# Attention scores of a two-layer trunk: from 128-row products of a stacked query to 64-row products on the two row halves of TensorE's array

## The chip, the cores and the metric

The kernel runs on one core of one Trainium2 chip. The metric is the device time of one execution in microseconds; a kernel's time is the median of its runs. The engines are TensorE (PE, with its weight loads listed apart as PEld), VectorE (DVE), ScalarE (ACT), GpSimd (POOL) and SyncE (SP), which issues the DMAs.

## The reference

Two layers on x of 1024 positions by 1024 channels. Each layer computes x + W_out(mixer(RMSNorm(x)) * silu(gate)), and one input projection gives q, k, v and the gate. Layer A is sliding-window attention (16 query heads, 2 key heads, window 128, a sink per head). Layer B runs three dilated sliding windows, (window, dilation) = (128,1), (512,4), (2048,16), each with 16 query heads and 4 key heads of its own, and merges them by their softmax denominators. Heads have 64 dims. The scores are, in blocks of 128 positions, queries of a block against keys of the block and of the one before it:

```python
s = jnp.einsum('nbqgrd,nbkgd->nbgrqk', qb, kk, preferred_element_type=jnp.float32) * SCALE
valid = (dist >= 0) & (dist <= max_dist) & ((blk > 0) | (j >= BLOCK))
p = jnp.exp(s - m[..., None])
```

## The kernel before

All matrix products run in float32r, with every operand split into a high part (rounded to float32r) and a low part (the rest), so that a product of two float32 operands becomes three float32r products (high·high, high·low, low·high): `mm3`, line 434. Transposes run in float32 on TensorE against an identity.

**Units.** The attention is made of 128 units, one for four query heads of one key head and one block of 128 positions: 32 in layer A (four groups of heads `n`, eight blocks) and 96 in layer B (four groups `n`, three dilations `g`, eight blocks). 72 of them see two key blocks (256 keys) and 56 see one (128 keys): the first block of a sequence, and all units of dilation 16, where two sequences of 64 share a block. A unit is `prep` (line 482: norm, rotation on POOL, transposes into `pq`, splitting of query and key) and `attend` (line 528: scores, softmax, transposes of the probabilities into `ptt`, product with v into `po`).

**Scores.** `prep` writes the query into `qs` with the high part of a head in partitions 0 to 63 and its low part in 64 to 127, by two ACT and two DVE instructions on 64 partitions each (even heads, odd heads). The key `kd` (`akr` in layer A, `kring` in layer B) holds the same 64 dims twice, in both partition halves, once as a high and once as a low copy. So a product with 128 rows gives (q_high + q_low)·k, and two of them, with k_high and k_low, give the score. With two key blocks these are two matmuls of 256 columns into one PSUM region. With one key block there is a single matmul of 256 columns, high and low copy side by side, and a DVE addition (`pe<-pss,con`) adds one half to the mask before the reduction reads the other. The tile `pss` is one PSUM bank and holds two heads; each unit takes two of them in turn (`NB["pS"]` is 2). A DVE reduction per head (listed as CUSTOM_DVE) adds the mask, scales and takes the minimum of the negated scores; ACT takes the exponential.

**What sets the order.** `Plan` (line 97) records all instructions in program order with an estimated duration from `_cost` (line 245), and `issue` (line 191) then orders them by a list scheduler: on each engine, of the instructions whose operands are there by its estimate, the one earliest in program order (with biases). The projections (`psz`, `psg` for the gate, `psw` for W_out) thus fill what the attention leaves of TensorE. Every instruction is issued from one recording helper, line 286, so all rows of the profile bear that line, and tiles tell them apart.

Of the kernel before, what the change touches and what calls it, by code (L numbers as in the profile page):

```python
# [12 lines left out]
F32 = mybir.dt.float32  # L13
F32R = mybir.dt.float32r
AF = mybir.ActivationFunctionType
OP = mybir.AluOpType
AX = mybir.AxisListType.X

P = 128
# [4 lines left out]
HD = 64  # L24
# [29 lines left out]
NB = {"pz": 2, "pS": 2, "pT": 2, "pO": 1, "pM": 1}  # L54
# [40 lines left out]


class Plan:
    """Records the instructions in program order, then issues them engine by engine in the order
    that a list scheduler finds: of the instructions whose operands are there, the earliest in
    program order first, so that the projections fill what the attention leaves of TensorE."""  # L100

    ENGINES = ("PE", "ACT", "DVE", "POOL", "SP")
    LAT = {("PE", "PE"): 0, ("PE", "ACT"): 200, ("PE", "DVE"): 200, ("PE", "POOL"): 200, ("PE", "SP"): 200,
# [141 lines left out]
def _cost(eng, name, out, ins):  # L245
    n = out.free_size()
    if eng == "PE":
        if name == "transpose":
            return 109
        return 213 if n < 2 * P else n / 2.4 + 3  # L250
    if eng == "SP":
        return out.size() * 4 / 300.0
    if eng == "DVE":
        if name == "tensor_reduce":
            n = ins[0].free_size()
        if name == "reciprocal":
            return 60 + 6.5 * n
        if name == "tensor_scalar":
            return 130 + 0.53 * n
        return (140 if name in ("tensor_tensor_reduce", "scalar_tensor_tensor") else 70) + 1.04 * n  # L260
    if eng == "ACT":
        return (60 if len(ins) == 1 else 160) + 0.84 * n
    return 150 + 2.1 * n
# [27 lines left out]
def trunk(ctx, tc, x, norm_a, w_in_a, q_gain_a, k_gain_a, sinks_a, w_out_a,  # L291
          norm_b, w_in_b, q_gain_b, k_gain_b, w_out_b, xt, const, out):
    nc = Plan(tc)
    x, out = x[0], out[0]
# [11 lines left out]
    pS = pool("ps", NB["pS"], space=PS)  # L306
# [4 lines left out]
    def f(ap):  # L311
        return ap.bitcast(F32)

# [1 line left out]
    ident = nc.tile(cp, [P, P], F32, name="ident")  # L315
    make_identity(tc.nc, ident)
    con = nc.tile(cp, [P, CS_W + 6 * P], F32, name="con")
# [7 lines left out]
    rows = nc.tile(sp, [16, P], F32, tag="zi", bufs=3, name="rows")  # L325
# [19 lines left out]
    gc = gt[:, 16:24].rearrange("p (a b) -> p a b", a=2)  # L345
# [22 lines left out]
    x1d = tc.dram_tile([T, D], F32, name="x1d")  # L368
    xpd = tc.dram_tile([T, D], F32, name="xpd")

# [1 line left out]
    def split(hi, lo, src, g=None, sub=nc.vector):  # L372
        if g is None:
            nc.scalar.activation(hi, src, AF.Copy)
            sub.tensor_tensor(lo, src, f(hi), op=OP.subtract)
        else:
            nc.scalar.activation(hi, src, AF.Copy, scale=g)
            nc.vector.scalar_tensor_tensor(lo, src, g, f(hi), op0=OP.mult, op1=OP.subtract)
# [103 lines left out]
    def prep(kind, order, tpos, z, nh, kv, slot):  # L482
        w = nh * HD
        sq = nc.tile(sp, [P, 320], F32, tag="sq", bufs=1, name="sq")
        nc.gpsimd.tensor_tensor(sq[:, :w], z[:, :w], z[:, :w], op=OP.mult)
        ss = nc.tile(sp, [P, 5], F32, tag="ss", bufs=2, name="ss")
        nc.vector.tensor_reduce(ss[:, :nh], sq[:, :w].rearrange("p (h d) -> p h d", d=HD), axis=AX, op=OP.add)
        r = nc.tile(sp, [P, 5], F32, tag="r", bufs=3, name="r")
        rstd(r[:, :nh], ss[:, :nh], 1.0, HD * EPS)
        zr = z[:, :w].rearrange("p (h d) -> p h d", d=HD)[:, :, :ROT]  # L490
        t0 = nc.tile(sp, [P, 5, ROT], F32, tag="t0", bufs=1, name="t0")[:, :nh]
        t1 = nc.tile(sp, [P, 5, ROT], F32, tag="t1", bufs=1, name="t1")[:, :nh]
        nc.gpsimd.tensor_tensor(t0, zr, rg[:, kind, :nh], op=OP.mult)
        c_, s_ = cs[:, order, tpos, 0], cs[:, order, tpos, 1]
        nc.gpsimd.tensor_tensor(t1, t0, c_[:, None, :].to_broadcast([P, nh, ROT]), op=OP.mult)
        hf = ROT // 2
        nc.gpsimd.tensor_tensor(zr[:, :, :hf], t0[:, :, hf:],
                                s_[:, None, :hf].to_broadcast([P, nh, hf]), op=OP.mult)
        nc.gpsimd.tensor_tensor(zr[:, :, hf:], t0[:, :, :hf],
                                s_[:, None, hf:].to_broadcast([P, nh, hf]), op=OP.mult)  # L500
        nc.gpsimd.tensor_tensor(zr, zr, t1, op=OP.add)
        pm = nc.tile(pM, [P, 4, P], F32, tag="m", bufs=NB["pM"], name="pq")
        for pr in range(2):
            nc.tensor.transpose(pm[:, pr], z[:, pr * P:(pr + 1) * P], ident)
        qs = nc.tile(sp, [P, 2, 2, P], F32R, tag="qs", bufs=2, name="qs")
        gq = gc[:, 0, kind:kind + 1]
        for two in range(2):
            rows = slice(two * HD, two * HD + HD)
            nc.scalar.activation(qs[:HD, :, two], pm[rows, 0:2], AF.Copy, scale=gq[rows])
            nc.vector.scalar_tensor_tensor(qs[HD:, :, two], pm[rows, 0:2], gq[rows], f(qs[:HD, :, two]),  # L510
                                           op0=OP.mult, op1=OP.subtract)
        if kv is not None:
            kd, vt = kv
            kh, kl = kd[:, 0], kd[:, 1]
            kk = nc.tile(sp, [P, 2, HD], F32, tag="kk", bufs=2, name="kk")
            nc.gpsimd.tensor_scalar(kk, z[:, None, 4 * HD:5 * HD].to_broadcast([P, 2, HD]), r[:, 4:5], -8.0,
                                    op0=OP.mult, op1=OP.mult)
            nc.tensor.transpose(pm[:, 2], kk.rearrange("p a b -> p (a b)"), ident)
            gk = gc[:, 1, kind:kind + 1]
            nc.scalar.activation(kh[:, slot], pm[:, 2], AF.Copy, scale=gk)  # L520
            nc.vector.scalar_tensor_tensor(kl[:, slot], pm[:, 2], gk, f(kh[:, slot]),
                                           op0=OP.mult, op1=OP.subtract)
            zv = z[:, 5 * HD:6 * HD]
            nc.scalar.activation(vt[:, slot, :HD], zv, AF.Copy)
            nc.gpsimd.tensor_tensor(vt[:, slot, HD:], zv, f(vt[:, slot, :HD]), op=OP.subtract)
        return qs, r

    def attend(qs, r, kv, slots, mask, nm, l, sink, o_even, o_odd):
        flush()
        kd, vt = kv  # L530
        nb = len(slots)
        W = nb * P
        if nb == 2:
            st = slots[1] - slots[0]
            ks = [kd[:, s, slots[0]:slots[1] + 1:st] for s in range(2)]
        pe = nc.tile(sp, [P, 4, 2 * P], F32, tag="p", bufs=2, name="pe")
        for pr in range(2):
            ps = nc.tile(pS, [P, 2, 2 * P], F32, tag="s", bufs=NB["pS"], name="pss")
            for two in range(2):
                if nb == 2:  # L540
                    nc.tensor.matmul(ps[:, two], qs[:, pr, two], ks[0], start=True, stop=False)
                    nc.tensor.matmul(ps[:, two], qs[:, pr, two], ks[1], start=False, stop=True)
                else:
                    nc.tensor.matmul(ps[:, two], qs[:, pr, two], kd[:, :, slots[0]], start=True, stop=True)
            if nb == 1:
                nc.vector.tensor_tensor(pe[:, 2 * pr:2 * pr + 2, P:], ps[:, :, P:],
                                        mask[:, None, :].to_broadcast([P, 2, P]), op=OP.add)
            for two in range(2):
                h = 2 * pr + two
                nc.vector.tensor_tensor_reduce(out=pe[:, h, :W], in0=ps[:, two, :W],  # L550
                                               in1=mask if nb == 2 else pe[:, h, P:], op0=OP.add,
                                               op1=OP.min, scale=r[:, h:h + 1], scalar=3e38,
                                               accum_out=nm[:, h:h + 1])
        if sink is not None:
            nc.vector.tensor_tensor(nm, nm, sink, op=OP.min)
        for h in range(4):
            nc.scalar.activation(pe[:, h, :W], pe[:, h, :W], AF.Exp, bias=nm[:, h:h + 1], scale=-1.0,
                                 accum_out=l[:, h:h + 1])
# [11 lines left out]
        for two, dst in ((0, o_even), (1, o_odd)):  # L570
            for d, sl in dst:
                a = po[:HD].rearrange("p (pr two q) -> p pr two q", pr=2, two=2)[:, :, two]
# [80 lines left out]
            nc.sync.dma_start(zi[sl, :width], view(zd))  # L653
        return zi

    # ================= layer A =================
    hT = [alloc_h(j) for j in range(4)]
    hB = {}

# [87 lines left out]
    for n in range(4):  # L747
# [5 lines left out]
        if n == 0:  # L753
            zd = tc.dram_tile([T, width], F32, name="za0")
            for t in range(NT):
# [12 lines left out]
                pr = nc.tile(pM, [P, 4, P], F32, tag="m", bufs=NB["pM"], name="pr")  # L768
# [8 lines left out]
            pr = nc.tile(pM, [P, 4, P], F32, tag="m", bufs=NB["pM"], name="pr")  # L777
# [13 lines left out]
        if n == 3:  # L791
            nc.bias = WOA
            y = load_y(0, 0, range(4), sub=YA)
# [5 lines left out]
        for t in range(NT):  # L799
# [7 lines left out]
            qs, r = prep(0, 0, t, z, 5 if n % 2 == 0 else 4, kv if n % 2 == 0 else None, t)  # L807
            sk = nsink[:, 4 * n:4 * n + 4]
            nm = nc.tile(sp, [P, 4], F32, tag="nm", bufs=2, name="nm")
            l = nc.tile(sp, [P, 4], F32, tag="l", bufs=2, name="l")  # L810
            slots = [t - 1, t] if t else [0]
            mask = mask_a[:, P:3 * P] if t else mask_a[:, :P]
# [15 lines left out]
    w0 = out_a_whole((6, 7))  # L828
    hT = hB

    # ================= layer B =================
    kk = nc.tile(sp, [P, 2, 4, P], F32R, tag="v2", bufs=1, name="kring")
    kring = [kk, nc.tile(sp, [P, 4, P], F32R, name="vring")]
    ucount = [0]
# [86 lines left out]
    for n in range(4):  # L921
        og, stn = {}, {}
        for g in (2, 1, 0):
            w = w0 if n == 0 and g == 2 else w_b(g, n)
            zd = bounce(hT, w, 384, f"zb{g}_{n}")
            if g == 0 and n == 3:
# [6 lines left out]
                y = first_y(0)  # L933
# [63 lines left out]
```

## Time and profile before

| | before |
|---|---|
| median of 3 runs | 1298.51 us (1296.77 to 1298.76) |
| span of the profiled execution | 1295.1 us |
| PE busy | 1257.3 us, 97%, 7851 matmuls |
| PEld busy | 1132.2 us, 87% |
| DVE busy | 1032.6 us, 80% |
| ACT busy | 867.9 us, 67% |
| POOL busy | 703.6 us, 54% |

A matmul's duration in the profile runs from its start to its modelled end, and matmuls overlap, so durations add up to more than the engine's time. What a matmul costs the stream is the distance from its start to the start of the next one. In the timeline view, equal instructions in a row stand as one row with their count.

### The profile page before, as it was taken

What the parts mean: (1) busy time and instruction counts of PE and PEld (TensorE: products, weight loads), DVE (VectorE), ACT (ScalarE), POOL (GpSimd) and SP (SyncE); (2) the same over time, 40 slices, a digit from 0 to 9 for tenths busy, and PEclk for the clock granted to TensorE, in tenths of its full rate; (3) what the DMA queues carried; (4) which work ended last, traced back from release to release, by engine and by line L of the source; (5) the groups of instructions that cost most, each with busy time, mean ns of one, the idle gap of its engine ahead of it and who ended that gap; (6) DMA issues with size and microseconds to landing.
All of it is one profiled execution on the core that took longest, in us unless ns stands there. A gap on an engine that the chain in (4) does not pass through costs nothing. (4 is left out here: it accounts for less than half of the span.)

```text
span 1295.1 us, 25655 instructions
## 1 busy us (share of the span) xinstructions
PE 1257.3 (97%) x7851; PEld 1132.2 (87%) x7851; DVE 1032.6 (80%) x2968; ACT 867.9 (67%) x2365; POOL 703.6 (54%) x1388
## 2 busy tenths in 40 slices
PE   6999999999999999999999999999999999999998
PEld 5999999998778999988889988889988888887777
DVE  8778778777965338778888888988778888779995
ACT  4376766767653347877757877767877767887760
POOL 4764455446410046555577656577556566587621
PEclk9999999999999999999999999999999999999999
DMA  7423223346254133223334323334223344354544
GB/s 242 128 76 110 77 85 102 91 161 185 83 166 142 66 112 100 82 62 105 117 112 128 88 74 94 107 106 137 82 69 106 98 124 133 117 156 135 165 141 157
DMA packets 142666, 149.74 MB, mean 116 GB/s; under 512 B 33576, under 2 KB 129344, under 8 KB 142528
## 3 DMA queue, kind: packets, MB, share of 16 engines
q1 hardware_dynamic: 142528, 148.09, 37.3%
q8 instruction: 63, 1.03, 0.3%
q14 instruction: 75, 0.61, 0.2%
HBM read 105.57 MB, written 42.47 MB: 114 GB/s over the span
## 5 line engine op out<-in xcount | busy, mean ns | idle before, releaser
L286 PE MATMUL psz<-wt,hT 128*128 128x384 f32 (+1 forms) x3072 | 640.9, 344 | 6.1 <-ACT wt L286 3.9
L286 PEld LDWEIGHTS psz<-wt,hT 128*128 128x128 f32 x3072 | 512.9, 191 | 14.8 <-ACT wt L286 4.0
L286 PE MATMUL psg<-hT,wt 128*128 128x256 f32 x1536 | 226.0, 291 | 0.0
L286 ACT ACTIVATE pe<-pe,st 128x128 f32<-128x128 f32 (+1 forms) x384 | 169.5, 443 | 59.8 <-DVE st L286 57.4
L286 PEld LDWEIGHTS psg<-hT,wt 128*128 128x128 f32 x1536 | 203.9, 192 | 2.7
L286 PE MATMUL ptt<-ident,pe 128*128 128x128 f32 x800 | 177.3, 281 | 6.2 <-ACT pe L286 5.4
L286 DVE SCALAR_TENSOR_TENSOR qs<-pq,gt,qs 64x256 fp32r<-64x256 f32 x256 | 123.8, 484 | 42.4 <-ACT qs L286 36.0
L286 POOL TENSOR_TENSOR r<-r,ex 128x5 f32<-128x5 f32 (+1 forms) x128 | 152.8, 1194 | 5.9
L286 ACT ACTIVATE qs<-pq,gt 64x256 fp32r<-64x256 f32 x256 | 120.1, 469 | 46.2 <-PE pq L286 41.0
L286 DVE TENSOR_TENSOR pp<-ptt,pp 128x512 fp32r<-128x512 f32 x200 | 131.7, 685 | 20.9 <-ACT pp L286 18.1
L286 POOL TENSOR_TENSOR sq<-zi 128x320 f32<-128x320 f32 (+1 forms) x128 | 93.4, 730 | 88.0 <-DMA zi<-zb 41.1
L286 PEld LDWEIGHTS ptt<-ident,pe 128*128 128x128 f32 x800 | 104.6, 140 | 39.8 <-ACT pe L286 23.6
L286 DVE CUSTOM_DVE_ANT_0 pe<-pss,con,r 128x256 f32<-128x256 f32 x288 | 127.7, 476 | 10.5 <-PE pss L286 8.7
L286 ACT ACTIVATE oh<-po 64x512 f32<-64x512 f32 x128 | 76.1, 595 | 81.3 <-PE po L286 79.8
L286 DVE SCALAR_TENSOR_TENSOR wt<-raw,gt,wt 128x384 fp32r<-128x384 f32 (+1 forms) x188 | 109.9, 615 | 23.8 <-ACT wt L286 22.6
L286 POOL TENSOR_SCALAR r<-ss 128x5 f32<-128x5 f32 (+1 forms) x128 | 31.1, 243 | 179.3 <-DVE st L286 96.4
L286 ACT ACTIVATE pp<-ptt 128x512 fp32r<-128x512 f32 x200 | 111.5, 594 | 19.2 <-PE ptt L286 18.0
L286 PE MATMUL po<-pp,vring 128*128 128x512 f32 x280 | 107.7, 413 | 2.4 <-DVE pp L286 1.8
L286 PE MATMUL psw<-hT,wy 128*128 128x512 f32 x384 | 105.7, 405 | 0.0
L286 ACT ACTIVATE wt<-raw,gt 128x384 fp32r<-128x384 f32 (+1 forms) x188 | 100.0, 564 | 6.4 <-PE psw L286 2.4
L286 PE MATMUL pss<-kring,qs 128*128 128x256 f32 x560 | 94.3, 285 | 0.8 <-DVE kring L286 0.6
L286 PEld LDWEIGHTS pss<-kring,qs 128*128 128x128 f32 x560 | 84.4, 188 | 9.8 <-DVE kring L286 3.1
(142 smaller groups left out, 2115.6 us busy)
## 6 DMA issues: line engine op xcount, KB each, us to landing
raw<-in_w_in_b_dram SPq DMA_DIRECT2D x96, 192.0 KB
zb<-z SPq DMA_DIRECT2D x96, 192.0 KB
cb<-cd SPq DMA_DIRECT2D x128, 128.0 KB
zi<-zb SPq DMA_DIRECT2D x64, 192.0 KB
raw<-in_w_in_a_dram SPq DMA_DIRECT2D x48, 128.0 KB
yraw<-yd SPq DMA_DIRECT2D x24, 256.0 KB
zi<-zb SPq DMA_DIRECT2D x64, 96.0 KB
xt<-in_xt_dram SPq DMA_DIRECT2D x16, 256.0 KB
```

The lines of the kernel that those rows point to most:

```text
L286: self.plan.add(self.name, method, lambda: fn(*args, **kw), outs, ins, dur, func)
```

## The change

- `prep`: the high parts of all four heads go into `qs[:, 0]` and the low parts into `qs[:, 1]`, by one ACT and one DVE instruction on 128 partitions. An even head lies in partitions 0 to 63, an odd one in 64 to 127.
- `attend`: a head's score is three products with 64 rows: (q_high, k_high), (q_high, k_low), (q_low, k_high). Even and odd head alternate, on rows 0 to 63 and on rows 64 to 127, and write different `pss` tiles (`ps[two]`, which now holds the even or the odd heads of both pairs). With one key block a product has 128 columns, with two 256. The DVE addition of the one-block units is gone. Both `pss` tiles of a unit are taken before its first product.
- `_cost`: a matmul's estimate is max(108, n/2.4 + 13) instead of n/2.4 + 3 (213 under 256 columns). The orders below follow from this too.

Matmuls go from 7851 to 8587: 800 of the scores become 1536, 672 with 128 columns and 864 with 256, half of them with a tile of 64 rows at row 0 and half at row 64.

```diff
@@ _cost
-        return 213 if n < 2 * P else n / 2.4 + 3
+        return max(108, n / 2.4 + 13)
@@ prep
-        gq = gc[:, 0, kind:kind + 1]
-        for two in range(2):
-            rows = slice(two * HD, two * HD + HD)
-            nc.scalar.activation(qs[:HD, :, two], pm[rows, 0:2], AF.Copy, scale=gq[rows])
-            nc.vector.scalar_tensor_tensor(qs[HD:, :, two], pm[rows, 0:2], gq[rows], f(qs[:HD, :, two]),
-                                           op0=OP.mult, op1=OP.subtract)
+        split(qs[:, 0], qs[:, 1], pm[:, 0:2], gc[:, 0, kind:kind + 1])
@@ attend
-        if nb == 2:
-            st = slots[1] - slots[0]
-            ks = [kd[:, s, slots[0]:slots[1] + 1:st] for s in range(2)]
+        st = slots[-1] - slots[0] or 1
+        ks = [kd[:, i, slots[0]:slots[-1] + 1:st] for i in range(2)]
         pe = nc.tile(sp, [P, 4, 2 * P], F32, tag="p", bufs=2, name="pe")
+        ps = [nc.tile(pS, [P, 2, 2 * P], F32, tag="s", bufs=NB["pS"], name="pss") for _ in range(2)]
         for pr in range(2):
-            ps = nc.tile(pS, [P, 2, 2 * P], F32, tag="s", bufs=NB["pS"], name="pss")
-            for two in range(2):
-                if nb == 2:
-                    nc.tensor.matmul(ps[:, two], qs[:, pr, two], ks[0], start=True, stop=False)
-                    nc.tensor.matmul(ps[:, two], qs[:, pr, two], ks[1], start=False, stop=True)
-                else:
-                    nc.tensor.matmul(ps[:, two], qs[:, pr, two], kd[:, :, slots[0]], start=True, stop=True)
-            if nb == 1:
-                nc.vector.tensor_tensor(pe[:, 2 * pr:2 * pr + 2, P:], ps[:, :, P:],
-                                        mask[:, None, :].to_broadcast([P, 2, P]), op=OP.add)
...
+            for i, (x, y) in enumerate(((0, 0), (0, 1), (1, 0))):
+                for two in range(2):
+                    rows = slice(two * HD, two * HD + HD)
+                    nc.tensor.matmul(ps[two][:, pr, :W], qs[rows, x, pr], ks[y][rows], start=i == 0, stop=i == 2)
+        for h in range(4):
+            nc.vector.tensor_tensor_reduce(out=pe[:, h, :W], in0=ps[h % 2][:, h // 2, :W], in1=mask, op0=OP.add,
+                                           op1=OP.min, scale=r[:, h:h + 1], scalar=3e38,
+                                           accum_out=nm[:, h:h + 1])
```

On PE, the scores of the unit of layer A with n = 2 and t = 4 (two key blocks) stand like this before; `psz` is the projection of the next group, `pc` a transpose of 8 columns, `po` the product of the unit ahead with v:

```order
L286 MATMUL pss<-akr,qs 128x256 x2
L286 MATMUL psz<-wt,hT 128x256 x2
L286 MATMUL pc<-ident,rc 8x128
L286 MATMUL pss<-akr,qs 128x256 x2
L286 MATMUL po<-pp,akv 128x512
L286 MATMUL pss<-akr,qs 128x256 x4
```

and like this now (the pattern goes on to the twelfth score product):

```order
L286 MATMUL pss<-akr,qs 128x256
L286 MATMUL psg<-hT,wt 128x256
L286 MATMUL pc<-ident,rc 8x128
L286 MATMUL pss<-akr,qs 128x256
L286 MATMUL psg<-hT,wt 128x256
L286 MATMUL pss<-akr,qs 128x256
L286 MATMUL psg<-hT,wt 128x256
L286 MATMUL pss<-akr,qs 128x256
L286 MATMUL psg<-hT,wt 128x256
```

The eight score products stood in three stretches; the twelve now stand singly, each between two gate products of 128 rows.

On PE, the scores of the unit of layer B with n = 0, g = 1 and u = 4 (one key block) before, and what stands around them:

```order
L286 MATMUL psz<-wt,hT 128x384
L286 MATMUL po<-pp,vring 128x512
L286 MATMUL psz<-wt,hT 128x384
L286 MATMUL pss<-kring,qs 128x256 x4
L286 MATMUL pq<-ident,zi 128x128 x2
L286 MATMUL psz<-wt,hT 128x384 x14
```

and the same unit now:

```order
L286 MATMUL ptt<-ident,pe 128x128 x2
L286 MATMUL pss<-kring,qs 128x128 x2
L286 MATMUL psg<-hT,wt 128x256 x2
L286 MATMUL pss<-kring,qs 128x128 x4
L286 MATMUL po<-pp,vring 128x512
L286 MATMUL pss<-kring,qs 128x128 x5
L286 MATMUL po<-pp,vring 128x512 x2
L286 MATMUL pss<-kring,qs 128x128
L286 MATMUL po<-pp,vring 128x512
```

Four products in one stretch have become twelve of 128 columns in four stretches, with `psg` and `po` of 128 rows between them. Over the whole program PE's order has 232 stretches of score products before and 405 now, of which 93 are a single product, 117 have two, 64 four and 53 five.

## Rows read from the trace of the kernel before

**Rows 1.** The page, part 1 (busy, share, instructions) and part 2 (granted clock).
```profile
PE 1257.3 (97%) x7851; PEld 1132.2 (87%) x7851; DVE 1032.6 (80%) x2968; ACT 867.9 (67%) x2365; POOL 703.6 (54%) x1388
PEclk9999999999999999999999999999999999999999
```

**Rows 2.** Groups by shape, PE: tiles, shapes, count, busy us, mean ns, idle before.
```profile
L286 PE MATMUL psz<-wt,hT 128*128 128x384 f32 x2688 | 584.7, 351 | 6.1 <-ACT wt L286 3.9 <-DVE wt L286 1.9 <-ACT z L286 0.2
L286 PE MATMUL psg<-hT,wt 128*128 128x256 f32 x1536 | 226.0, 291 | 0.0
L286 PE MATMUL ptt<-ident,pe 128*128 128x128 f32 x800 | 177.3, 281 | 6.2 <-ACT pe L286 5.4
L286 PE MATMUL po<-pp,vring 128*128 128x512 f32 x280 | 107.7, 413 | 2.4 <-DVE pp L286 1.8 <-DVE og L286 0.4
L286 PE MATMUL psw<-hT,wy 128*128 128x512 f32 x384 | 105.7, 405 | 0.0
L286 PE MATMUL pss<-kring,qs 128*128 128x256 f32 x560 | 94.3, 285 | 0.8 <-DVE kring L286 0.6
...
L286 PE MATMUL psz<-wt,hT 128*128 128x256 f32 x384 | 56.2, 289 | 0.0
...
L286 PE MATMUL pss<-akr,qs 128*128 128x256 f32 x240 | 43.9, 295 | 2.1 <-DVE akr L286 0.6 <-DVE qs L286 0.6 <-ACT pe L286 0.6
```

**Rows 3.** Timeline, PE, layer A: start us, length, tiles, count; projections up to a transpose.
```profile
34.17 1.73 PE L286 MATMUL psz<-wt,hT 128*128 128x384 f32 x9
35.73 0.27 PE L286 MATMUL pr<-ident,sr 128*128 128x128 f32 x1
```

**Rows 4.** Timeline, PE, layer A: gate products, with an 8-column transpose (pc) among them.
```profile
206.42 0.27 PE L286 MATMUL pc<-ident,rc 128*8 128x128 f32 x1
206.45 0.96 PE L286 MATMUL psg<-hT,wt 128*128 128x256 f32 x6
207.24 0.39 PE L286 MATMUL po<-pp,akv 128*128 128x512 f32 x1
207.47 0.28 PE L286 MATMUL psg<-hT,wt 128*128 128x256 f32 x1
207.59 0.38 PE L286 MATMUL pq<-ident,zi 128*128 128x128 f32 x2
207.73 0.60 PE L286 MATMUL psg<-hT,wt 128*128 128x256 f32 x3
208.16 0.63 PE L286 MATMUL po<-pp,akv 128*128 128x512 f32 x2
```

**Rows 5.** Timeline, PE, layer B: the four score products of a one-block unit.
```profile
711.48 0.64 PE L286 MATMUL pss<-kring,qs 128*128 128x256 f32 x4
711.95 0.38 PE L286 MATMUL pq<-ident,zi 128*128 128x128 f32 x2
```

**Rows 6.** Timeline, PE then PEld: the transpose with 16 rows (pg) among projections.
```profile
48.44 1.03 PE L286 MATMUL psz<-wt,hT 128*128 128x384 f32 x5
49.40 0.23 PE L286 MATMUL pg<-ident,rows 16*128 16x16 f32 x1
49.56 0.96 PE L286 MATMUL psz<-wt,hT 128*128 128x384 f32 x4
50.36 0.27 PE L286 MATMUL pr<-ident,ra 128*8 128x128 f32 x1
...
49.40 0.13 PEld L286 LDWEIGHTS pg<-ident,rows 16*128 16x128 f32 x1 [0.25 <-issue]
49.56 0.64 PEld L286 LDWEIGHTS psz<-wt,hT 128*128 128x128 f32 x4
```

**Rows 7.** Groups by shape, ACT and DVE: what the change removes or halves.
```profile
L286 ACT ACTIVATE qs<-pq,gt 64x256 fp32r<-64x256 f32 x256 | 120.1, 469 | 46.2 <-PE pq L286 41.0 <-DVE qs L286 1.5
...
L286 DVE SCALAR_TENSOR_TENSOR qs<-pq,gt,qs 64x256 fp32r<-64x256 f32 x256 | 123.8, 484 | 42.4 <-ACT qs L286 36.0
...
L286 DVE TENSOR_TENSOR pe<-pss,con 128x256 f32<-128x256 f32 x112 | 43.8, 417 | 15.9 <-PE pss L286 15.8
```

More of the change, by code (lines that the diff above doesn't have):

```diff
@@ L532, in attend @@
         W = nb * P
-        if nb == 2:
-            st = slots[1] - slots[0]
-            ks = [kd[:, s, slots[0]:slots[1] + 1:st] for s in range(2)]
+        st = slots[-1] - slots[0] or 1
+        ks = [kd[:, i, slots[0]:slots[-1] + 1:st] for i in range(2)]
         pe = nc.tile(sp, [P, 4, 2 * P], F32, tag="p", bufs=2, name="pe")
+        ps = [nc.tile(pS, [P, 2, 2 * P], F32, tag="s", bufs=NB["pS"], name="pss") for _ in range(2)]
         for pr in range(2):
-            ps = nc.tile(pS, [P, 2, 2 * P], F32, tag="s", bufs=NB["pS"], name="pss")
-            for two in range(2):
-                if nb == 2:
-                    nc.tensor.matmul(ps[:, two], qs[:, pr, two], ks[0], start=True, stop=False)
-                    nc.tensor.matmul(ps[:, two], qs[:, pr, two], ks[1], start=False, stop=True)
-                else:
-                    nc.tensor.matmul(ps[:, two], qs[:, pr, two], kd[:, :, slots[0]], start=True, stop=True)
-            if nb == 1:
-                nc.vector.tensor_tensor(pe[:, 2 * pr:2 * pr + 2, P:], ps[:, :, P:],
-                                        mask[:, None, :].to_broadcast([P, 2, P]), op=OP.add)
[L548 to L553, printed above, removed]
+            for i, (x, y) in enumerate(((0, 0), (0, 1), (1, 0))):
[6 more added lines that the diff above has]
+                                           accum_out=nm[:, h:h + 1])
         if sink is not None:
```

## The prediction

> **What bounds the kernel now.** I read the page's busy shares first: TensorE is busy 97% of the span, VectorE 80%, ScalarE 67%, and the granted clock is at its upper level, 2.4 GHz, in every slice [rows 1]. So a microsecond on PE is a microsecond of the kernel unless it falls into a wait, and work taken from DVE or ACT counts only where PE waits for it.
>
> A busy share does not tell what a matmul costs, because matmuls overlap. The timeline does, by the distance from one start to the next. Nine projections of 384 columns run from 34.17 to 35.73: 0.173 us each [rows 3]. In the next strip a gate product of 256 columns costs 0.12 (207.47 to 207.59) and a product of 512 columns 0.23 (207.24 to 207.47). Two transposes of 128 columns and three gate products take 0.57 (207.59 to 208.16), which leaves 0.105 for a transpose [rows 4]. The four score products of 256 columns take 0.47, again 0.12 each [rows 5].
>
> With these prices and the counts by shape [rows 2] the PE stream adds up: 2688 x 0.173 = 465; (1536 + 384) x 0.12 = 230; 800 score products x 0.12 = 96; products of 512 columns, 280 + 384 in the two groups shown and 504 in smaller ones, 1168 x 0.23 = 269; transposes, 800 ptt and 475 in smaller groups, 1275 x 0.105 = 134. The sum is 1194 us. The profiled execution's span is 1295.1, so only 101 us are waits, the start of the program among them. The median of the runs is 3.4 us above that span; I add this at the end.
>
> **The change, part by part.**
>
> *Score products.* Before: 96 us. After: 1536 products, 672 of 128 columns and 864 of 256. No row shows two products on different row halves. One bound: the two run one after the other, each at the full price. A 128-column matmul is nearest to the transposes (0.105, the same load of 128 columns and the same stream), so 672 x 0.105 + 864 x 0.12 = 174, that is +78. Other bound: the even and the odd head run side by side, and a pair costs what one costs. What the rows show of this is that PE can start a matmul 0.03 us behind another (206.42 to 206.45 [rows 4]), so issuing would not forbid it; and the two use other partitions and other PSUM tiles. I take side by side, as nothing they use is shared. But a pair only forms where both stand in one stretch. By the order after the change, the 405 stretches hold 371 pairs or singles of 128 columns and 482 of 256 (half of each stretch's length, rounded up; 768 would be all in pairs). That is 371 x 0.105 + 482 x 0.12 = 97, so **+1 us** against 96. The saving that six pairs for eight products promise is eaten by odd stretches and by 128-column products, which cost nearly as much as those of 256. Bounds of the 128-column price: 0.067 if it is all stream (the step from 256 to 384 columns is 0.053), -14 us; 0.213, the estimate in the kernel's table before, +40 us.
>
> *Changing between 128-row and 64-row products.* Every stretch is entered from a 128-row matmul and left to one. Before there is no such change, but for two transposes at the start. One stands in a running stream: `pg`, 16 rows. Nine projections and pg take 1.92 us (48.44 to 50.36); nine projections are 1.56, so pg costs 0.36 [rows 6]. A transpose with all 128 rows and only 8 columns of weights, pc, costs 0.10 (206.42 to 207.24 less six gate products [rows 4]). So entering and leaving a row tile costs about 0.25 us on top of the matmul. The weight-load rows show how: pg's load starts only at 49.40, with 0.25 us idle before it that no semaphore ends, and the next projection's load waits until 49.56, instead of running under the matmul ahead [rows 6]. In the changed order there are 405 stretches: 405 x 0.25 = **+101 us**. Lower bound 0: pc changes the width of the tile in columns, not in rows, and pays nothing. I take 0.25, since pg's row is the nearest: it too narrows the tile in rows, by the same instruction.
>
> The Trainium skill, TensorEngine Tiling (Array Packing), section Key Properties, says that a change of the tiling mode, not merely of the tile, drains TensorE, and that different tiles load and multiply in parallel. By the drain alone the sum stays at +101 as pg's row gives it; pc's row contradicts the rule for tiles narrowed in columns, and by that row the sum would be 0. That two tiles work in parallel no run here shows yet.
>
> *ScalarE and VectorE.* Query split: 256 ACT instructions of 0.469 and 256 DVE ones of 0.484 become 128 each on twice the partitions with the same 256 columns, so -60 us of ACT and -62 us of DVE. The DVE addition of the one-block units goes: 112 x 0.417 = -47 us [rows 7]. None of this bounds: ACT falls from 868 to 808 busy and DVE from 1033 to 924, beside PE's 1257 [rows 1]. It counts through PE's waits. With a tenth less work on DVE and the slower stream on PE, I let a third of the 101 us of waits go: **-35 us**, bounds 0 and -60 (the rest is the start and latency that the change leaves).
>
> *Order and buffers.* Both pss tiles are taken at a unit's start, so the next unit's scores wait for reductions of the third and fourth head, not of the second. With 128 units in 1295 us there is one in 10 us, and projections fill PE meanwhile; I put it at nothing. If that cover fails, a unit waits for about one DVE instruction of the size of the qs one, 0.48 us, 62 us in all. The longer estimates for projections move fillers: 147 W_out products stand behind the last score product before, 235 after. On a PE without gaps this costs nothing. DMAs and POOL instructions are the same in number.
>
> *Sum:* 1295.1 + 1 + 101 - 35 = 1362; with 3.4 us, **1366 us**.
>
> **The rivals.**
>
> *A: the change of row tiles is free, pairs overlap.* 1295.1 + 1 - 35 + 3.4 = **1265**. For it: pc's row, and pg is a single event in a stream of full-length ones. Against it: pg's load had no semaphore left to wait for and still stood idle. This is the case on the other side. It decides where a stretch costs under 34 / 405 = 0.08 us instead of 0.25; about there the kernel comes out unchanged.
>
> *D: the tile change costs as in pg, and the two halves don't overlap.* 78 instead of 1: 1295.1 + 78 + 101 - 35 + 3.4 = **1442**. For it: transposes of 128 columns never come closer than 0.105 on average though their stream is shorter, so weight loads seem to go one at a time; pg's load with 16 rows takes 0.13 us, hardly less than a full one, so 64 rows don't shorten it. If loads of the two halves queue, a pair of 128-column products costs 0.21.
>
> *C: no overlap, and free tile changes.* 1295.1 + 78 - 35 + 3.4 = **1342**.
>
> The Trainium skill, TensorE: Matmul & The Clock Gate, Part 3, The mechanism, says that weight loads overlap with matmuls in flight when the row group differs, and that tiles in different row groups run nearly at once. That speaks against C and D; no row here tests it, and without it the chances below would only move between my case and D.
>
> **How the numbers follow.** My case 0.42, A 0.27, D 0.17, C 0.09, and 0.05 for a cost per stretch near 0.08 us, where nothing moves. A difference under 0.2% is about what a measurement of this kernel cannot tell from no change. Faster by more than that is A: 0.27. Within 0.2%: 0.05. Slower: 0.42 + 0.17 + 0.09 = 0.68. The range: my case alone, with waits of 0 to -60 and the 128-column price of 0.067 to 0.213, is 1400.5 - 60 - 14 = 1326 to 1400.5 + 40 = 1440 (1400.5 being the sum without the term for the waits). The whole range reaches down through A's 1265 with 10 us of its own, to 1255, and up to 1440, which takes C and nearly half of D. Left out are the upper half of D, A below 1255, and little else, about 0.2.
>
> **What would show it.** In the profile after: the distance from the last 128-row matmul to the first of a stretch, and from the last of a stretch to the next, against 0.12 to 0.23; a weight load that starts only when the matmul ahead has ended (case A if it starts under it). Inside a stretch of ten or twelve: starts that come in pairs 0.12 us apart by the pair (mine and A) or singly 0.105 to 0.12 apart (C and D). In the single products between gate products of layer A, about 0.25 us for each besides the 0.12. ACT should show 128 qs instructions of about 0.47 us, DVE as many of about 0.48, and no `pe<-pss,con` addition. PE's idle time tells what the lighter engines gave. I am wrong if PE's stream of scores takes no longer than 96 us with its changes counted in, or if PE's own waits grow in place of shrinking.

## The result: 11% slower

| | before | after |
|---|---|---|
| median | 1298.18 us (1296.77 to 1298.76, 4 runs) | 1443.37 us (1443.07 to 1446.58, 4 runs) |
| span of the profiled execution | 1295.1 us | 1441.8 us |
| ratio to before | | 1.1122, 95% interval 1.1105 to 1.1138 |

The forecast was 1366 us, the range 1255 to 1440. The sign was right; the loss is 145 us where 68 were forecast.

The page of the changed kernel, parts 1 and 2 (busy, share, instructions; granted clock in 40 slices), to be read beside [rows 1]:

```profile
PE 1397.8 (97%) x8587; PEld 1167.9 (81%) x8587; DVE 926.9 (64%) x2728; ACT 798.7 (55%) x2237; POOL 697.4 (48%) x1388
...
PEclk9999999899999999999999999999999999999999
```

TensorE is 97% busy as before and has 140 us more of it; DVE has lost 106 us and ACT 69, as the change intends. The groups that answer to [rows 7] (ACT, then DVE: count, busy us, mean ns, idle before):

```profile
L286 ACT ACTIVATE qs<-pq,gt 128x256 fp32r<-128x256 f32 x128 | 60.7, 474 | 80.9 <-PE pq L286 78.8
...
L286 DVE SCALAR_TENSOR_TENSOR qs<-pq,gt,qs 128x256 fp32r<-128x256 f32 x128 | 61.2, 478 | 33.1 <-ACT qs L286 32.5
```

Half the instructions at the old duration (0.469 and 0.484 before), and the 112 additions of [rows 7] are gone. So the loss is PE's.

**Where PE's time went.** The timeline shows it, PE first (start us, length, tiles, count), then PEld, for one unit of layer B with two key blocks:

```profile
706.26 0.63 PE L286 MATMUL po<-pp,vring 128*128 128x512 f32 x2
706.82 0.38 PE L286 MATMUL pss<-kring,qs 64*128 64x256 f32 x1
707.14 0.50 PE L286 MATMUL po<-pp,vring 128*128 128x512 f32 x1
707.57 0.98 PE L286 MATMUL pss<-kring,qs 64*128 64x256 f32 x11
708.48 0.79 PE L286 MATMUL psz<-wt,hT 128*128 128x384 f32 x3
...
706.09 0.36 PEld L286 LDWEIGHTS po<-pp,vring 128*128 128x128 f32 x2
706.82 0.18 PEld L286 LDWEIGHTS pss<-kring,qs 64*128 64x128 f32 x1 [0.37 <-issue]
707.13 0.19 PEld L286 LDWEIGHTS po<-pp,vring 128*128 128x128 f32 x1
707.57 0.77 PEld L286 LDWEIGHTS pss<-kring,qs 64*128 64x128 f32 x11 [0.25 <-issue]
708.47 0.65 PEld L286 LDWEIGHTS psz<-wt,hT 128*128 128x128 f32 x4
```

Two readings. First, eleven products of 256 columns take 0.91 us (707.57 to 708.48), the exit included. Eleven times the 0.12 us that a product of 256 columns costs in [rows 4] would be 1.32: the two halves overlap. Second, a lone 64-row product takes 0.32 us (706.82 to 707.14) and the po between two stretches 0.43 (707.14 to 707.57; 0.23 in [rows 4]). At each change the weight load stands at the start of its own matmul instead of running under the matmul ahead, and at both entries after idle time that the profile calls issue (0.37 and 0.25 us).

The plainest strip lies in layer A, where single score products stand between single gate products:

```profile
272.08 0.39 PE L286 MATMUL psg<-hT,wt 128*128 128x256 f32 x1
272.40 0.38 PE L286 MATMUL pss<-akr,qs 64*128 64x256 f32 x1
272.71 0.38 PE L286 MATMUL psg<-hT,wt 128*128 128x256 f32 x1
273.02 0.38 PE L286 MATMUL pss<-akr,qs 64*128 64x256 f32 x1
273.33 0.38 PE L286 MATMUL psg<-hT,wt 128*128 128x256 f32 x1
```

Each of these matmuls takes 0.31 us from start to start; one of 256 columns costs 0.12 in [rows 4]. A change of the tile's rows costs 0.19 us, and a stretch has two of them.

I summed the distances between starts over both traces, at the prices of the prediction (0.105 us for 128 columns; 0.12, 0.173 and 0.226 for 256, 384 and 512). The first part is the time of the score products with what their stretches add at entry, at exit and to the one matmul behind; the second is what all other matmuls take above their price. Half clock is the time that PE spent at the lower of its two levels, 1.2 GHz; it lies inside the other two, and half of it is lost.

| us | before | after | difference |
|---|---|---|---|
| score stretches with their changes | 108.5 | 258.8 | +150.3 |
| waits elsewhere | 87.3 | 83.8 | -3.5 |
| of both: at half clock, end of program left out | 0 | 24 | |

The sum, +146.8, is the difference of the spans, 146.7, as it must be where every distance is counted once. The slots of the products alone (pairs and singles, as in the prediction) come to 96.6 us, so 405 stretches cost (150.3 - 0.9) / 405 = 0.37 us each where 0.25 was forecast. This is net: the score stretches before took 12.8 us more than their products' 95.7, and without taking that off it is 162.2 / 405 = 0.40. And PE's waits hardly fell where 35 us were forecast. The experiments ask three things: is it the tile change, does the overlap hold, and where did the 35 us stay.

### The profile page after: what moved, and what is told of

The parts are those of the page before. It is cut to its first block, busy times and chain, and to the rows that moved or that the text cites. A ratio compares the mean times of both kernels' runs of the same rounds, so it can differ in the third digit from the quotient of the medians.

```text
span 1441.8 us, 26772 instructions
## 1 busy us (share of the span) xinstructions
PE 1397.8 (97%) x8587; PEld 1167.9 (81%) x8587; DVE 926.9 (64%) x2728; ACT 798.7 (55%) x2237; POOL 697.4 (48%) x1388
## 4 chain that ended last, share of the span: by engine, by line
PE 73%; DVE 13%; ACT 7%; issue 3%; DMA 2%; POOL 2%; SPq 1%; ACTq 0%; DVEq 0%; POOLq 0%
PE psz L286 26%; PE psg L286 11%; PE psw L286 10%; PE pss L286 9%; PE po L286 7%; PE ptt L286 6%; PE pq L286 3%; DVE og L286 2%; DVE pe L286 2%; ACT pe L286 2%; DVE wt L286 2%; ACT oh L286 1%; DVE o L286 1%; DMA cb<-cd 1%; DVE pp L286 1%
## 5 line engine op out<-in xcount | busy, mean ns | idle before, releaser
L286 PE MATMUL psz<-wt,hT 128*128 128x384 f32 (+1 forms) x3072 | 630.5, 344 | 8.5 <-ACT wt L286 3.9
L286 DVE CUSTOM_DVE_ANT_0 pe<-pss,con,r 128x256 f32<-128x256 f32 (+1 forms) x512 | 194.5, 420 | 92.2 <-PE pss L286 89.3
L286 PE MATMUL psg<-hT,wt 128*128 128x256 f32 x1536 | 249.9, 301 | 0.0
L286 PEld LDWEIGHTS psg<-hT,wt 128*128 128x128 f32 x1536 | 209.5, 194 | 9.3 <-issue 1.3
L286 DVE SCALAR_TENSOR_TENSOR wt<-raw,gt,wt 128x384 fp32r<-128x384 f32 (+1 forms) x188 | 105.6, 600 | 76.7 <-ACT wt L286 76.5
L286 PEld LDWEIGHTS pss<-kring,qs 64*128 64x128 f32 x1152 | 91.3, 185 | 69.7 <-issue 47.0
L286 PE MATMUL pss<-kring,qs 64*128 64x128 f32 (+1 forms) x1152 | 137.2, 307 | 1.7 <-ACT kring L286 0.9
L286 PEld LDWEIGHTS ptt<-ident,pe 128*128 128x128 f32 x800 | 100.6, 140 | 39.0 <-ACT pe L286 24.4
L286 PE MATMUL po<-pp,vring 128*128 128x512 f32 x280 | 116.8, 445 | 4.0 <-DVE og L286 2.2
L286 ACT ACTIVATE qs<-pq,gt 128x256 fp32r<-128x256 f32 x128 | 60.7, 474 | 80.9 <-PE pq L286 78.8
L286 POOL TENSOR_SCALAR r<-ss 128x5 f32<-128x5 f32 (+1 forms) x128 | 30.0, 234 | 146.8 <-DVE nm L286 74.8
L286 DVE TENSOR_TENSOR og<-po,oh 64x128 f32<-64x128 f32 (+1 forms) x192 | 77.9, 455 | 25.8 <-ACT oh L286 22.8
```

The lines of the kernel that those rows point to most:

```text
L286: self.plan.add(self.name, method, lambda: fn(*args, **kw), outs, ins, dur, func)
```

## Experiments

A time without a ratio is from a single run.

### Fewer stretches: the twelve products joined

```diff
+        nc.batch = []
         for pr in range(2):
             for i, (x, y) in enumerate(((0, 0), (0, 1), (1, 0))):
...
+        nc.join()
```

Between the two lines the plan collects the twelve products as one entry.

> The changed kernel with the twelve score products of a unit recorded as one piece, so that nothing stands between them: 128 stretches of 64-row products in place of 405, the same products, prices and buffers. Theory (each entry to and exit from 64-row tiles costs, 0.37 us a stretch by the trace after): 1443 - 277 x 0.37 = 1341 us, between 1325 and 1350. Rival (the 64-row products themselves or their many weight loads are what is slow, or the pss tiles taken early make PE wait): within 20 us of 1443.

Measured: 1362.93 us, 80 less than the changed kernel, and above the 1325 to 1350 of the theory. The sums of its trace: stretches 143.9 us (after: 258.8), of which the products are 87.1 (all in pairs now), so 56.8 / 128 = 0.44 us a stretch; but waits elsewhere 117.9 (83.8). The rival is out. 22 us of the expected gain are missing because a unit's products, kept together, make PE wait more elsewhere: PEld's waits for the exponential (`ptt` for ACT `pe`) are 43.7 us there against 24.4.

PE's timeline of one such unit (one key block): twelve products of 128 columns in 0.82 us, 703.99 to 704.81, the way out of the tile included in part. At the transposes' 0.105 they would take 1.26 one by one.

```profile
703.99 0.89 PE L297 MATMUL pss<-kring,qs 64*128 64x128 f32 x12
704.81 0.74 PE L297 MATMUL po<-pp,vring 128*128 128x512 f32 x2
```

Cut off at 704.02, the same view has two of the twelve already:

```profile
703.99 0.33 PE L297 MATMUL pss<-kring,qs 64*128 64x128 f32 x2
```

The trace's single starts give the sign that the prediction named: over all 128 units the products come in pairs, the odd head 3 or 4 ns (median) behind the even one. A pair follows a pair after 0.11 us with 128 columns and 0.12 with 256; only the second pair comes later, 0.16 and 0.22 after the first.

### The same order with full rows

```diff
-                    rows = slice(two * HD, two * HD + HD)
+                    rows = slice(0, P)
```

> The changed kernel with every score product on all 128 rows (both heads' dims summed, so the scores are not the reference's): the order on PE, the number of products, loads and stretches are the same, but no tile ever changes and no two products can overlap. Theory (changing tiles costs 149 us, overlap saves 78): 1443 - 149 + 78 = 1372 us, between 1355 and 1380. Rival (the scattered order or the number of products costs, not the tile): 1443 + 78 = 1521 us, since only the overlap is lost.

Measured: 1379.86 us. PE's order is that of the changed kernel line by line, with the same 405 stretches and 1536 products; each product takes 128 rows, none is on a half of its own, and it is 64 us faster. The stretches take 197.6 us, 174 of them the price of 1536 products one by one; waits elsewhere are 81.3, as after (83.8). So neither the scattered order nor the number of products is the loss. It is the change of tile rows.

### A 64-row product by itself, in the kernel before

```diff
+            nc.tensor.matmul(ps[:, 0], qs[:HD, pr, 0], kd[:HD, :, slots[0]], start=True, stop=True)
             for two in range(2):
```

> The kernel before with two more score products per unit (256 in all), each of 64 rows and 256 columns, whose result the next product overwrites. By the order they stand in 234 stretches of 64 rows among 128-row matmuls. Theory (a stretch of 64 rows costs about 0.37 us besides its products, whatever else the change does): 1298 + 256 x 0.12 + 234 x 0.37 = 1415 us. Rival (64 rows alone cost nothing, the loss comes of the order and the waits): 1298 + 31 = 1329, the same as with 128-row products in their place.

> The same 256 additional products with all 128 rows. Both theories: 1298 + 31 = 1329 us; what the kernel with 64 rows takes more than this one is the price of the tile changes by itself.

 (here `:P` in place of `:HD`)

Measured: 1378.43 us with 64 rows, 1332.08 with 128. The same 256 products, on fewer rows, cost 46 us more: the tile change is dear outside this change too, and the rival is out. But 46 / 234 is 0.20 us a stretch, not 0.37, and 1415 was a miss. One unit of the run with 64 rows shows why the price is not wrong:

```profile
708.99 1.56 PE L286 MATMUL pss<-kring,qs 64*128 64x256 f32 x6
710.38 0.38 PE L286 MATMUL pq<-ident,zi 128*128 128x128 f32 x2
```

The six are two products of 64 rows and four of 128; they take 1.39 us where six times 0.12 is 0.72. Over the whole trace the 234 stretches of 64 rows add 91 us to their products and to the matmuls beside them, 0.39 each, as in the changed kernel before waits are taken off (0.40); of the 212 that are a single product four in five lie between 0.38 and 0.40. The time rises by only 46 us because 45 us of waits are gone: the waits elsewhere are 57.4 us against 77.4, and of the 27 us that the run with 128 rows has among its score products (153.7 us where 1056 x 0.12 is 126.7) about 2 are left. So a stretch costs the kernel its full 0.39 us only where PE would not have waited anyway.

### Even heads first, then odd heads

```diff
-        for pr in range(2):
-            for i, (x, y) in enumerate(((0, 0), (0, 1), (1, 0))):
-                for two in range(2):
...
+        for two in range(2):
...
+            for pr in range(2):
+                for i, (x, y) in enumerate(((0, 0), (0, 1), (1, 0))):
```

> As the kernel with the joined products, but the six of the even heads (rows 0 to 63) stand ahead of the six of the odd heads (rows 64 to 127): 128 stretches as well, but no two neighbours on different halves except at the middle. Theory (pairs overlap fully when they alternate): 78 us more than with the joined alternating products, about 1419. Rival (overlap brings nothing, the weight loads go one at a time): the same time as the joined alternating ones.

Measured: 1368.40 us, only 5 above the joined alternating kernel. That looks like the rival, but the trace says otherwise. Between the first and the last start of a stretch lie 126.9 us in all, against 88.4 with alternating halves and 160 if nothing overlapped (11 intervals of 0.105 or 0.12 in each of 56 and 72 units). One stretch of nine or more products of 128 columns starts at 701.87; its single starts lie 0.11 apart at first and 0.055 in the middle, where products of both halves run at once. So the overlap is about half lost, 38 us; waits elsewhere fell by 29 at the same time (117.9 to 89.1) and hid it. Its time alone shows neither that the order of the halves matters nor that it doesn't; the starts show that it does. That halves overlap is shown by the starts and the times per stretch above.

### The price rule alone

```diff
-        return 213 if n < 2 * P else n / 2.4 + 3
+        return max(108, n / 2.4 + 13)
```

> The kernel before with the new matmul price alone. Theory (PE has hardly any gaps, so the order matters little): 1298 us within 10. Rival (the new price pulls fillers to the end and PE's waits grow): 1310 to 1320.

Measured, in the kernel before: 1338.24 us, ratio 1.0304 (1.0287 to 1.0321). The theory falls; the rival holds in kind, 18 us beyond its range. It is one rule in the scheduler's table, no instruction more or less, and 40 us. No product of the kernel before has fewer than 256 columns, and transposes have a price of their own, so only the step from + 3 to + 13 acts. Behind the last score product 199 W_out products stand in this trace, 147 before. Waits elsewhere rise from 87.3 to 120.3 us, stretches from 108.5 to 117.0. PEld's waits (engine, tile, what it waited for: us, times, longest) before and with the new price:

```profile
PEld ptt L286 <- ACT pe L286: 23.6, 66, 1.8
PEld pq L286 <- issue: 10.9, 38, 0.8
PEld po L286 <- DVE pp L286: 9.5, 25, 0.8
```

```profile
PEld ptt L286 <- ACT pe L286: 39.9, 113, 2.3
PEld pq L286 <- issue: 17.4, 52, 0.9
PEld po L286 <- DVE pp L286: 12.0, 36, 1.4
```

PE comes more often, 113 times instead of 66, to a transpose whose exponential isn't done. That fits a scheduler to which each projection seems 0.01 us longer: it believes that ACT and DVE get further in that time, and puts what depends on them earlier in PE's order. This reading of the cause is argued; the order and the waits are what is shown.

### The price rule in the changed kernel, whole and in parts

> The changed kernel with the price rule of before, nothing else undone; by the order 348 stretches of 64-row products instead of 405. Theory (the new price makes PE wait here as it did alone, 35 to 40 us, and a stretch costs 0.37): 1443 - 38 - 57 x 0.37 = 1384 us, PE's waits outside the stretches down from 84 to about 50 us. Rival (the waits of the price only showed where DVE and ACT were full; they are lighter here): 1443 - 21 = 1422, waits unchanged.

Measured with the whole old rule: 1450.05 us. No gain at all, and waits elsewhere up from 83.8 to 109.8: against the theory, and above the rival's 1422 too. The old rule has two parts, and the next two runs undo them one by one.

> The changed kernel with matmuls priced at max(108, n/2.4 + 3): of the new price rule only the step from + 3 to + 13 is undone, the 128-column price stays at 108; 394 stretches of 64-row products by the order, against 405. Theory (the step to + 13 makes PE wait about 40 us here as it did in the kernel before, 1298 to 1338, and in the joined one, 1324 to 1363): 1443 - 40 - 11 x 0.37 = 1399 us, between 1390 and 1410. Rival (in this kernel the step costs nothing; the old rule as a whole gave 1450): 1435 to 1450.

Measured with max(108, n/2.4 + 3): 1401.13 us, 42 less than the changed kernel. Stretches 246.4 us (394 of them), waits elsewhere 53.6.

> The changed kernel with 213 for matmuls under 256 columns and n/2.4 + 13 above: of the new price rule only the 128-column price is undone; 370 stretches. Theory (the 213 makes the scheduler think one-block units twice as long on PE as they are, and is what made the old rule lose here): 1443 - 35 x 0.37 + 40 = 1470 us or more. Rival (the 128-column price doesn't matter): 1443 - 13 = 1430.

Measured with 213 under 256 columns: 1486.78 us, 43 more; waits elsewhere 132.5.

So the price rule is a loss of some 40 us here too, in its step from + 3 to + 13: 30 of the 42 us are waits elsewhere, 12 lie in the stretches. About 10 of the 42 are the clock, which is at the lower level for 24 us in the changed kernel and for 3.4 with the step undone. The rule's other part, 108 for products of 128 columns that the rule before had at 213, saves about as much; some 5 of these 43 us are the clock (34 us at the lower level with 213), and why the rest is saved no run shows. PEld's waits in the changed kernel and with the step undone:

```profile
PEld pss L286 <- issue: 65.3, 251, 0.4
PEld ptt L286 <- ACT pe L286: 24.4, 58, 1.9
```

```profile
PEld pss L286 <- issue: 64.1, 250, 0.4
PEld ptt L286 <- ACT pe L286: 14.6, 37, 1.9
```

> The kernel with joined products (1363 us) with matmuls priced at max(108, n/2.4 + 3). Theory (a new order alone moves the time by tens of us, in either direction, and tile changes stay 128 stretches): between 1330 and 1385. Rival (the low price returns the 40 us that the high one cost alone): 1323.

Measured: the joined kernel falls from 1362.93 to 1324.28 us, the rival's 1323. Three kernels, the same step, 40, 42 and 39 us. The waits at `pss` called issue, which the timeline above has at the entries into 64-row tiles, are 0.4 us in the kernel before, and the step does not touch them.

### Lighter ACT and DVE, nothing else moved

```diff
+            nc.swap = nothing if two else lambda: tc.nc.scalar.activation(qs[:, :, 0], pm[:, 0:2], AF.Copy, scale=gq)
             nc.scalar.activation(qs[:HD, :, two], pm[rows, 0:2], AF.Copy, scale=gq[rows])
...
+                nc.swap = nothing
                 nc.vector.tensor_tensor(pe[:, 2 * pr:2 * pr + 2, P:], ps[:, :, P:],
...
```

The plan sees the old instructions; what is issued is the lighter one, or none.

> The kernel before with its own order on every engine, kept by planning the removed instructions and not issuing them: the query split in one ACT and one DVE instruction of 128 partitions per unit, and the DVE addition of the one-block units left out (the scores are then not the reference's). PE's stream is unchanged; ACT is 60 us lighter, DVE 109. Theory (lighter ACT and DVE give PE back a third of its waits, as the prediction had it, and the change lost that only through its new order): 1298 - 35 = 1263 us, between 1250 and 1275. Rival (PE's waits are latencies of single steps, not load): 1290 to 1298.

Measured: 1260.52 us, ratio 0.9709 (0.9691 to 0.9727): 37 us, where the prediction had 35. PE's 7851 matmuls stand in the same order; in the profiled execution, 4 us above the median, waits elsewhere fall from 87.3 to 62.4 us and the stretches' sum by 7. Its busy times and PEld's longest wait:

```profile
PE 1232.6 (98%) x7851; PEld 1139.4 (90%) x7851; DVE 926.3 (73%) x2728; ACT 803.1 (64%) x2237; POOL 707.8 (56%) x1388
```

```profile
PEld ptt L288 <- ACT pe L288: 15.1, 43, 1.8
```

It lays the query out as the changed kernel does, under score products that are made for the old layout, and leaves the addition out, so its scores mean nothing; it tells only what the lighter engines are worth.

### Other prices in the kernel before

> The kernel before with matmuls priced at n/2.4 - 7 instead of + 3 (a lower price in place of the change's higher one). Theory (the price is a margin: the cheaper PE looks to the scheduler, the later it puts what waits for ACT and DVE, and the fewer PE waits): below 1298 us, 1280 to 1295. Rival (1298 sits at the best price, and either step away costs): 1305 to 1330.

Measured with - 7: 1326.55 us, ratio 1.0216 (1.0199 to 1.0233). The theory of a margin falls. But 44 us of this run are at the lower clock level, which makes about 22 of the 28 us; without them it would be 1304, still not below 1298. PE, clock and DMA in three stretches (PE, PEld, DVE, ACT, POOL busy; PEclk; DMA share, GB/s):

```profile
1080.00:1089.00 9.00, 9.00 (x75) 8.79 (x74) 7.84 (x24) 5.31 (x16) 6.34 (x12) 1.00 0.33 99
1089.00:1110.00 21.00, 12.40 (x80) 9.98 (x79) 16.57 (x51) 11.16 (x34) 13.75 (x26) 0.81 0.57 170
1110.00:1130.00 20.00, 16.25 (x72) 13.10 (x72) 14.17 (x49) 15.80 (x40) 12.37 (x27) 0.68 0.21 64
```

PE was fully busy up to 1089, then had 8.6 us idle of 21, and the granted clock fell, 0.81 over that stretch and 0.68 over the next. By these two rows some 20 us ran at the lower level, which is another 10 us lost on top of the 8.6.

> The kernel before with matmuls priced at n/2.4 + 1 instead of + 3, a step too small to mean anything. Theory (any new order loses what this one was tuned to have, up to 40 us, whichever way the price moves): 1305 to 1330 us. Rival (the price itself acts, in proportion): 1298 within 5.

The kernel has + 1, as its text says, not the + 5 of its label. Measured: 1303.47 us, between the theory's range and the rival's.

> The kernel before with matmuls priced at n/2.4 + 5 instead of + 3. Theory (any new order loses): 1305 to 1330 us. Rival (in proportion to the 40 us that + 13 cost): 1298 + 8 = 1306.

Measured with + 5: 1312.29 us, at a granted clock of 0.93 over the first 145 us, which is most of the 14 us. The theory that any new order loses tens of us is not borne out by steps of 2; of the steps of 10, the one up cost 40 us and the one down 28, most of it clock. Nothing here beats the kernel before.

## Why the prediction was wrong in size

**The score products: right.** +1 us was forecast for the products in their slots, by overlapping pairs; the slots of the order come to 96.6 us against 95.7, and the pairs 3 or 4 ns apart and the times of whole stretches (0.91 us for eleven products, 0.82 for twelve) are only possible with overlap. Rival D's number, 1442, is nearly what was measured, but D's mechanism, halves that don't overlap, is not what happened, and rival C's neither.

**The change of tile rows: right mechanism, mis-sized.** 405 x 0.25 = 101 us was forecast; it measured 0.37 a stretch net, 149 us, of which the lower clock makes at most 12. The row was the right one, the reading was not. From pg's 0.36 us in [rows 6] I took off 0.105, the price of a transpose in the stream. But that price, as I now read it, is mostly a weight load where loads follow each other; at a change the load stands exposed and is itself part of the cost. What pg streams is 16 columns, by an estimate from the same prices about 0.02 us (16 / 2.4 ns and the 13 ns that 256 and 384 columns pay on top). 0.36 - 0.02 = 0.34 us was there to be read, 138 us for the 405 stretches; the 0.05 us from there to the 0.39 of the lone products stays open. The drain rule of the Trainium skill, TensorEngine Tiling (Array Packing), section Key Properties, agrees with the changed kernel's trace (0.19 us for each of two changes) and with the run on full rows; its second half, that different tiles load and multiply in parallel, is now shown for tiles of different rows by the stretches above. That pc's row contradicts the rule, as the prediction says, does not follow: no row shows that pc is a change of the mode at all. Rival A fell with this.

**The relief: right by itself, not delivered.** -35 us was forecast and waits elsewhere fell by 3.5. With the order held, the lighter ACT and DVE give 37 us, and with the step of the price undone the changed kernel's waits are 53.6, 33.7 below before. So the term was sized right, though its third of the waits was a guess with no row behind it, and the match is in part luck. Another term that I had at nothing took it back: the price rule, "On a PE without gaps this costs nothing". PE had gaps of 101 us, and one number in the table moved the time by 40 us, 33 of them waits outside the stretches. This is the step of the prediction that failed by kind and not by size. The buffers, at nothing beside it, held: of the waits of score products the traces put 0.4 us on DVE's reductions (`pe`, `nm`) in the changed kernel and 3.5 in the joined one, where 62 were the worst case.

By these terms: 1298 + 1 (products) + 149 (changes of tile) - 37 (lighter engines) + 40 (step of the price) = 1451 us, against 1443 measured. The terms are from different kernels and not strictly additive; 8 us is what they leave open. The signs of the steps, and the side of the forecast, held; the two errors, 48 and some 32 us, are both on the side of too little loss.

## What to carry to other kernels

A tile of fewer rows halves nothing if it has to be entered and left between full-row matmuls: count the stretches in the issued order, not the products, and charge each with a load that can't run ahead, less what PE would have waited there anyway. When an edit changes a scheduler's estimate along with the work, measure the estimate alone first; here it moved as much as the lighter engines gave. And when a price is read from a rare row, ask which part of that row's time is already the thing to be priced.

## What the runs showed of the hardware

- Two matmuls on rows 0 to 63 and 64 to 127 run side by side in float32r, weight loads included: twelve products of 128 columns in 0.82 us, in pairs that start 3 or 4 ns apart and follow each other after 0.11 us, and still partly (126.9 us of starts against 88.4 and 160) when six of one half stand ahead of six of the other.
- A change between 128-row and 64-row tiles costs 0.19 us each way in a strip of single products of 256 columns, and a single 64-row product among 128-row ones 0.39 us in all. A transpose with 8 columns of weights (pc) pays nothing to be seen in [rows 4].
- In the strip of single products the granted clock fell to the lower level while PE was listed as busy throughout. Stretches of the changed kernel (columns as above):

```profile
266.00:270.00 4.00, 4.00 (x33) 3.76 (x32) 2.18 (x6) 2.59 (x8) 0.03 (x1) 1.00 0.13 31
270.00:274.00 4.00, 4.00 (x21) 2.64 (x19) 3.81 (x9) 2.04 (x6) 3.37 (x8) 1.00 0.29 88
274.00:284.00 10.00, 10.00 (x31) 7.15 (x31) 3.40 (x13) 2.49 (x4) 0.53 (x3) 0.55 0.13 40
284.00:290.00 6.00, 6.00 (x48) 6.00 (x47) 1.90 (x5) 5.56 (x11) 3.59 (x4) 0.90 0.52 145
```

  From 271 us on, PE alternated single products, 21 matmuls in 4 us instead of 33; from 274 to 284 the clock is 0.55, and the products are 0.51 us apart instead of 0.31. All stretches at the lower level together are 24 us in this run, so some 12 us of the loss; the changed kernel with the old step has 3.4 us of them.
